# Low weight parts of a trunk block in one tile per 512 columns, each copied and loaded when the unit two places up has used it; the last norm's sum folded and moved up one unit

## The chip, the cores and the metric

The kernel runs on one core of one Trainium2 chip. The metric is device time in microseconds of one execution, from its first to its last instruction and what lies around them. Engines are called by the names of the profile: PE (TensorE, matmuls), PEld (its weight loads), DVE (VectorE), ACT (ScalarE), POOL (GpSimd), SP (SyncE, which issues most loads).

## The reference

One layer of a hybrid decoder on 528 tokens (16 learned ones and 512 of the input), width 1024:

```
h  = concat(meta, x)
p  = rmsnorm(h, norm1_g) @ w_in              # q k v glr r u ga gb
o  = rmsnorm(gla_chunked(q, k, v, log_a), gla_norm_g)
y_a = (o * silu(r)) @ w_a
y_b = (group_matmul(multiscale_pool(u)) * pool_scale) @ w_b
h  = h + (sigmoid(ga + b) * y_a + sigmoid(gb + b) * y_b) @ w_o
a, bv = split(causal_dwconv(rmsnorm(h, norm2_g) @ w_up))
h  = h + (silu(a) * bv) @ w_down             # D_FF = 2816
out = rmsnorm(h, final_norm_g)[16:]
```

All is float32. What matters here: the many weight matrices, and the norm at the very end, which needs the sum of squares over all 1024 channels of a token before anything can be stored.

## The kernel before

**Three products for one.** Each float32 operand of a matmul is split into a high part, rounded to the `F32R` type, and a low part, the rest; a product is high x high, high x low and low x high, three matmuls. Activations are stored with channels on the 128 partitions and tokens along the row. Weights come as units: a unit is 128 partitions x 4 blocks x 512 columns (a block holds four 128x128 weights).

**Order of units.** A list `seq` holds the units of the second phase (from about 187 us): u, a, ga, gb, grp, b, o, up and down, in an order written by hand. The first phase (q, k, v, r and the attention) has its own weights and is not touched. There are three kinds of units:

- *plain* (`plain`, `plain_half`): all three products of 256 output channels, in two halves `c` of 48 matmuls. Half 0 uses blocks 1 and 2 of the direct weights, half 1 block 0 and the weights of block 3 (`x`).
- *fast* (`fast`, `seven`): the same output by seven block products for eight (a Strassen-like scheme), each product twelve matmuls. Three use blocks 2, 0 and 1 of the direct weights (in this order: first, third, fifth product), four use sums of blocks (`sa`, `sb`, made by `make_sums`). The evictions to `z` stand on ACT and DVE between them.
- *down* (`down`): six or four weights for each of two output tiles.

**How a unit's weights are made.** SP loads the raw unit (`fetch`, three buffers, 1 MB). For unit n+1, during unit n, ACT makes the high part of three blocks (`make_high`, L631) and the sums are formed on DVE and split (`make_sums`, L650, L284, L285). The low part is made in one of two ways. For down, grp, b and o (`split_here`) DVE subtracts the high part from the raw one (L285, L633). For all others (`make_low`) ACT copies the negative of the *raw* three blocks, rounded, into the low tile (L621, one instruction of 128x1536), and then POOL issues three DMAs that add the exact weights to it from HBM, one per block (L623, `accum_op=ALU.add`). Low and high tiles have two buffers each, so the low tile of unit n+2 takes the place of unit n's; the copy must wait until PE has read that one. `make_low(n + 2)` is called from `prepare(n)` at the end of unit n, in fast units behind the eviction `turned` (L758) on ACT's queue.

Within an engine the instructions run in the order that the tile framework's scheduler gives them, which follows the order of the program and its own estimate of when each could start; `tc.issue_after` puts an instruction behind a given one on its engine.

**The end.** The last four down units (part 3 of D_FF) are computed for two halves of the tokens, `CUTS` of 256 columns, one after the other: for each `i` of four, two accumulations (`pe` L992), the addition to `h` (L1056, DVE), the square (L1057, ACT), the sum of squares `tot` (L1061, DVE) and the scaling with the norm's weights (L1066). `finish` of a half then sums over partitions with four matmuls against a float32 matrix of ones (`n3s`, L1029; two for `tot`, which holds two channel tiles side by side, two for the last square), makes the reciprocal root (L267, L269 on ACT, L271 to L273 on DVE), scales four pairs of tiles (L1036, DVE) and stores them. The first half's `finish` is called in the second half's loop at `i == 1`, the second's at the end.

Of the kernel before, what the change touches and what calls it, by code (L numbers as in the profile page):

```python
# [78 lines left out]
def hybrid_block(ctx: ExitStack, tc: tile.TileContext, xt, g1d, wts, wsq, wdown, wglr, wgk, vecs, out):  # L79
# [515 lines left out]
    def direct_tiles(n):  # L595
        if n not in own:
            fetch(n)
            job = seq[n]
            if n >= len(seq) - 2:
                hl = two(f"{n}")  # L600
                own[n] = hl, [t.rearrange("p a k n -> p (a k n)") for t in hl], 1024
                return own[n]
            hl = [gp.tile([P, 3, 512], F32R, tag=f"g{c}", name=f"g{c}{n}") for c in "hl"]
            if job[0] == "down":
                k = 2 * PARTS[job[1]][1] * P
                hl = [t.rearrange("p a b -> p (a b)")[:, 0:k] for t in hl]
                own[n] = [t.rearrange("p (c k n) -> p c k n", c=2, n=P) for t in hl], hl, k
            else:
                own[n] = [blocks(t) for t in hl], hl, None
# [5 lines left out]
    def make_low(n):  # L615
        if n >= len(seq) or split_here(n) or n in low_made:
            return
        low_made.add(n)
        _, (hi, lo), _ = direct_tiles(n)
        kind, name, i = seq[n]  # L620
        act.activation(lo, loaded[n][:, 0:3], AF.Copy, scale=-1.0)  # L621
        for b in (2, 0, 1) if kind == "fast" else (0, 1, 2) if name == "grp" else (1, 2, 0):
            pool.dma_start(lo[:, b], wsq[UNIT[name] + i, :, b], accum_op=ALU.add)  # L623

    def make_high(n):
# [3 lines left out]
        _, (hi, lo), k = direct_tiles(n)  # L629
        if k is None:  # L630
            act.activation(hi, loaded[n][:, 0:3], AF.Copy)  # L631
            if split_here(n):
                dve.tensor_tensor(lo, loaded[n][:, 0:3], f32(hi), ALU.subtract)  # L633
        else:
            split(hi, lo, loaded[n].rearrange("p a b -> p (a b)")[:, 0:k])
# [25 lines left out]
    def behind(ins, made, n):  # L661
        if ins is None:
            return made(n)
        with tc.issue_after(ins.ins):
            made(n)
# [12 lines left out]
    def plain_half(n, i, c, xh, xl, cols, w):  # L678
        g, x = w
        accs = [bank(f"pp{n}_{c}{h}") for h in range(2)]  # L680
        for k in range(KT):
            w = [
                (x[e][:, 0, k // 2] if k % 2 else g[e][:, 0, k // 2]) if c
                else g[e][:, 2 if k % 2 else 1, k // 2]
# [10 lines left out]
    def plain(n, i, xh, xl, cols, evict, cross=None):  # L695
# [3 lines left out]
        for c in range(2):  # L699
# [3 lines left out]
            elif cross is None or cross[0] is CROSS_X:  # L703
                spare(2)
        prepare(n)
# [14 lines left out]
    def seven(acc, w, block, x, at, n, first=True):  # L720
        for k in range(4):
            for e, (a, b) in enumerate(((0, 0), (0, 1), (1, 0))):
                pe.matmul(  # L723
                    acc[:, 0:n], w[a][:, block, k], x[k][b][:, at],
# [10 lines left out]
    def fast(n, z, sides, cols):  # L735
        direct, crossed = sides
        g, sa, sb = weights(n)
# [412 lines left out]
```

## Time and profile before

| | us |
|---|---|
| median of 3 runs (lowest, highest) | 831.64 (830.6, 833.38) |
| profiled execution | 833.59 |
| its span, first to last instruction | 831.8 |
| PE busy | 816.0 |
| DVE busy | 595.6 |
| ACT busy | 479.1 |
| POOL busy, 114 of its 149 instructions the DMA issues of L623 | 122.5 |

Busy time is the time in which an engine had an instruction running; the matmuls of PE overlap and their ends are modelled. The list of waits names for each idle stretch of an engine the instruction that waited, the one that released it, the total, the count and the longest. A timeline row has the start, the duration, the engine, the line and the operands, and in brackets how long the engine sat idle before. "To landing" is the time from a DMA's issue to its data having arrived.

### The profile page before, as it was taken

The numbers are of one execution on the slowest core, as the hardware profiler recorded it, in microseconds if no ns is written. First come the engines' busy times: TensorE is split into PE (matmuls) and PEld (weight loads), VectorE is DVE, ScalarE is ACT, GpSimd is POOL, SyncE is SP. The second block draws the span as 40 slices with busy tenths as digits, with TensorE's granted clock in tenths as the row PEclk, the third lists the DMA queues.
The fourth block names the chain that finished last, engine by engine and source line by source line (L and its number), as shares of the span: only waits on it lengthen the run. The fifth ranks groups of instructions, "written<-read, shape, count | busy, mean of one in ns | idle before, by whom it ended". The sixth has DMA issues, their size and how long they took to land.

```text
span 831.8 us, 15134 instructions
## 1 busy us (share of the span) xinstructions
PE 816.0 (98%) x6311; PEld 789.9 (95%) x6311; DVE 595.6 (72%) x891; ACT 479.1 (58%) x686; POOL 122.5 (15%) x149
## 2 busy tenths in 40 slices
PE   9999999999999999999999999999999999999995
PEld 7999999999999999999999999999989988999894
DVE  7677346679756797755564598998759965899845
ACT  7297244586655676644234457774557734786643
POOL 5000000021222122110003322220122110320000
PEclk9999999999999999999999999999999999999998
DMA  6423220248667777734342756875557644775102
GB/s 224 152 77 100 78 76 27 112 106 239 168 133 167 173 178 177 197 84 152 109 153 99 173 117 157 180 153 156 146 140 164 160 111 155 159 171 140 51 26 102
DMA packets 35861, 113.17 MB, mean 136 GB/s; under 512 B 3952, under 2 KB 7024, under 8 KB 29776
## 3 DMA queue, kind: packets, MB, share of 16 engines
q1 hardware_dynamic: 18688, 81.79, 29.9%
q0 software_dynamic: 16416, 29.89, 21.9%
q8 instruction: 49, 0.80, 0.4%
q10 hardware_dynamic: 688, 0.53, 0.2%
q14 instruction: 20, 0.16, 0.1%
HBM read 110.10 MB, written 2.10 MB: 135 GB/s over the span
## 4 chain that ended last, share of the span: by engine, by line
PE 84%; DMA 5%; DVE 5%; ACT 2%; issue 1%; POOL 1%; SPq 1%; DVEq 0%; ACTq 0%
PE pp L689 18%; PE x L723 14%; PE pd L992 12%; PE q L723 9%; PE pv L173 6%; PE y L723 5%; PE v L723 5%; PE pr L173 4%; DMA gl<-in_wsq_dram 4%; PE pq L173 3%; PE pe L992 2%; PE pgrp L851 1%; PE po L485 1%; PE po L484 1%; ACT gl L621 1%
## 5 line engine op out<-in xcount | busy, mean ns | idle before, releaser
L623 POOL DMA_DIRECT2D gl<-in_wsq_dram x114 | 102.0, 1212 | 500.0 <-ACT gl L621 430.2
L631 ACT ACTIVATE gh<-raw 128x1536 fp32r<-128x1536 f32 x47 | 69.8, 1486 | 61.4 <-PE pp L689 26.6
L650 DVE TENSOR_TENSOR raw<-raw 128x512 f32<-128x512 f32 x116 | 79.9, 689 | 26.8 <-ACT gh L631 14.5
L992 PE MATMUL pd<-g,gh 128*128 128x512 f32 x288 | 89.8, 393 | 0.0
L992 PEld LDWEIGHTS pd<-g,gh 128*128 128x128 f32 x288 | 53.8, 188 | 12.2
L621 ACT ACTIVATE gl<-raw 128x1536 fp32r<-128x1536 f32 x38 | 56.2, 1479 | 9.0 <-issue 4.5
L992 PE MATMUL pd<-g,gl 128*128 128x512 f32 x144 | 56.7, 394 | 0.0
L156 ACT ACTIVATE whi<-wraw 128x1024 fp32r<-128x1024 f32 (+2 forms) x28 | 26.1, 934 | 50.9 <-PE pv L173 25.8
L157 DVE TENSOR_TENSOR wlo<-wraw,whi 128x1024 fp32r<-128x1024 f32 (+2 forms) x28 | 32.0, 1145 | 5.7 <-ACT whi L156 4.5
L977 ACT ACTIVATE cv<-z,vec 128x512 f32<-128x512 f32 x44 | 33.9, 812 | 0.0
L992 PEld LDWEIGHTS pd<-g,gl 128*128 128x128 f32 x144 | 27.0, 188 | 6.1
L978 DVE SCALAR_TENSOR_TENSOR cv<-z,vec,cv 128x512 f32<-128x512 f32 x44 | 32.2, 746 | 0.0
L979 DVE SCALAR_TENSOR_TENSOR cv<-z,vec,cv 128x512 f32<-128x512 f32 x44 | 32.2, 746 | 0.0
L1017 DVE TENSOR_TENSOR h<-pd,h 128x512 f32<-128x512 f32 x24 | 16.5, 689 | 20.2 <-PE pd L992 20.0
L285 DVE TENSOR_TENSOR gl<-raw,gh 128x1536 fp32r<-128x1536 f32 (+1 forms) x14 | 23.5, 1679 | 6.1 <-ACT gh L284 6.1
L173 PE MATMUL pv<-xh,whi 128*128 128x264 f32 x128 | 26.3, 287 | 0.0
L173 PE MATMUL pr<-xh,whi 128*128 128x258 f32 (+1 forms) x128 | 25.9, 284 | 0.0
L173 PE MATMUL pv<-xl,whi 128*128 128x264 f32 x128 | 25.9, 283 | 0.0
L173 PE MATMUL pv<-xh,wlo 128*128 128x264 f32 x128 | 25.9, 283 | 0.0
L173 PE MATMUL pr<-xh,wlo 128*128 128x258 f32 (+1 forms) x128 | 25.8, 283 | 0.0
L173 PE MATMUL pr<-xl,whi 128*128 128x258 f32 (+1 forms) x128 | 25.6, 281 | 0.0
L284 ACT ACTIVATE gh<-raw 128x1536 fp32r<-128x1536 f32 (+1 forms) x14 | 19.9, 1422 | 5.1 <-PE pd L992 3.2
(1279 smaller groups left out, 2980.7 us busy)
## 6 DMA issues: line engine op xcount, KB each, us to landing
raw<-in_wsq_dram SPq DMA_DIRECT2D x47, 1024.0 KB, 5.7
gl<-in_wsq_dram POOLq DMA_DIRECT2D x114, 256.0 KB, 7.3
wraw<-in_wts_dram SPq DMA_DIRECT2D x22, 512.0 KB, 3.7
raw<-in_wdown_dram SPq DMA_DIRECT2D x12, 768.0 KB, 4.3
xb<-in_xt_dram SPq DMA_DIRECT2D x4, 528.0 KB, 5.1
h<-in_xt_dram SPq DMA_DIRECT2D x4, 514.0 KB, 5.1
raw<-in_wdown_dram SPq DMA_DIRECT2D x4, 512.0 KB, 3.5
x<-in_xt_dram SPq DMA_DIRECT2D x7, 264.0 KB, 5.6
```

The lines of the kernel that those rows point to most:

```text
L157: dve.tensor_tensor(lo[:, a:b], t[:, a:b], f32(hi[:, a:b]), ALU.subtract)
L173: pe.matmul(acc[:, s, : b - a], w, x[:, a:b], start=(i == 0 and w is wh and x is xh), stop=(i == n - 1 and last),)
L621: act.activation(lo, loaded[n][:, 0:3], AF.Copy, scale=-1.0)
L623: pool.dma_start(lo[:, b], wsq[UNIT[name] + i, :, b], accum_op=ALU.add)
L631: act.activation(hi, loaded[n][:, 0:3], AF.Copy)
L650: dve.tensor_tensor(raw[:, dst], raw[:, dst], raw[:, x], ALU.add)
L689: pe.matmul(acc[:, 0 : b - a], w[p], q[k][:, a:b], start=k == 0 and e == 0, stop=k == KT - 1 and e == 2,)
L723: pe.matmul(acc[:, 0:n], w[a][:, block, k], x[k][b][:, at], start=first and k == 0 and e == 0, stop=k == 3 and e == 2, skip_group_check=no ...
L977: act.activation(cv, z[:, c, META:], AF.Identity, scale=v1("cw2", m), bias=v1("cb", m))
L978: dve.scalar_tensor_tensor(cv, z[:, c, META - 1 : L - 1], v1("cw1", m), cv, ALU.mult, ALU.add)
L979: dve.scalar_tensor_tensor(cv, z[:, c, META - 2 : L - 2], v1("cw0", m), cv, ALU.mult, ALU.add)
L992: pe.matmul(acc, w[p][:, c, k], gated[k0 + k][q][:, a:b], start=k == 0 and e == 0, stop=k == nk - 1 and e == 2,)
```

## The change

Four edits, the first three for the low parts.

1. The low tile becomes three tiles of one block each (`gl0`, `gl1`, `gl2`, two buffers each, the same bytes in all); the weights are handed on as a function `piece(e, b, k)` in place of an array. Where DVE makes the low part, it does so in one subtraction per block (three instructions of 512 columns, two in the last part), and a down unit's two tiles are cut out of the blocks.
2. `make_low` takes the blocks to be made as an argument. Each block gets its own copy on ACT (128x512) and its own DMA right behind it, where before one copy of 128x1536 stood ahead of three DMAs.
3. In a fast unit n, block 2 of unit n+2 is made behind the eviction of `q` (L748), block 0 behind that of the second `x` (L751), and the rest in `prepare` as before; in a plain unit blocks 2 and 1 after half 0, block 0 in `prepare`.
4. At the end the sums of squares are folded into one tile: three further additions of 256 columns on DVE for the first half, two for the second. `finish` then has one matmul with the ones for the first half and two for the second, where both had four. The first half's `finish` is called at `i == 0`.

```diff
-            hl = [gp.tile([P, 3, 512], F32R, tag=f"g{c}", name=f"g{c}{n}") for c in "hl"]
...
+            hi = gp.tile([P, 3, 512], F32R, tag="gh", name=f"gh{n}")
+            lo = [gp.tile([P, 512], F32R, tag=f"gl{b}", name=f"gl{b}_{n}") for b in range(3)]
+            nk = PARTS[job[1]][1] if job[0] == "down" else 4
+
+            def piece(e, b, k):
+                b, k = divmod(b * nk + k, 4)
+                t = lo[b] if e else hi[:, b]
+                return t[:, k * P : (k + 1) * P]
...
-    def make_low(n):
-        if n >= len(seq) or split_here(n) or n in low_made:
+    def make_low(n, order=(2, 1, 0)):
+        if n >= len(seq) or split_here(n):
             return
-        low_made.add(n)
-        _, (hi, lo), _ = direct_tiles(n)
-        kind, name, i = seq[n]
-        act.activation(lo, loaded[n][:, 0:3], AF.Copy, scale=-1.0)
-        for b in (2, 0, 1) if kind == "fast" else (0, 1, 2) if name == "grp" else (1, 2, 0):
-            pool.dma_start(lo[:, b], wsq[UNIT[name] + i, :, b], accum_op=ALU.add)
+        lo = direct_tiles(n)[2]
+        for b in order:
+            if (n, b) not in low_made:
+                low_made.add((n, b))
+                act.activation(lo[b], loaded[n][:, b], AF.Copy, scale=-1.0)
+                pool.dma_start(lo[b], wsq[UNIT[seq[n][1]] + seq[n][2], :, b], accum_op=ALU.add)

     def make_high(n):
...
+        nb = -(-2 * PARTS[seq[n][1]][1] // 4) if seq[n][0] == "down" else 3
+        act.activation(hi[:, 0:nb], loaded[n][:, 0:nb], AF.Copy)
+        if split_here(n):
+            for b in range(nb):
+                dve.tensor_tensor(lo[b], loaded[n][:, b], f32(hi[:, b]), ALU.subtract)
...
@@ def plain
+            if c == 0:
+                make_low(n + 2, (2, 1))
         prepare(n)
...
@@ def fast
-        act.activation(z22, q[:, n_], AF.Copy)
+        behind(act.activation(z22, q[:, n_], AF.Copy), make_low, n + 2, (2,))
         seven(v_, g, 0, crossed, 3, w)
         seven(x, sa, 1, crossed, 2, w, False)
-        act.activation(z12, x[:, n_], AF.Copy)
+        behind(act.activation(z12, x[:, n_], AF.Copy), make_low, n + 2, (0,))
...
-    def finish(part, a, b, tot, last):
+    def finish(part, a, b, parts):
...
-        for e, x in enumerate((tot[:, 0], tot[:, 1], last[:, 0], last[:, 1])):
-            pe.matmul(s3[:, 0:w], ones32, x, start=e == 0, stop=e == 3)
+        for e, x in enumerate(parts):
+            pe.matmul(s3[:, 0:w], ones32, x, start=e == 0, stop=e == len(parts) - 1)
...
-            if i == 1 and late:
+            if i == 0 and late:
                 finish(*late)
...
+            if i == 2:
+                dve.tensor_tensor(tot[:, 0], tot[:, 0], tot[:, 1], ALU.add)
+            if i == 3:
+                dve.tensor_tensor(tot[:, 0], tot[:, 0], sq[:, 0], ALU.add)
...
-        late = part, a, b, tot, sq
+        if part < len(CUTS) - 1:
+            dve.tensor_tensor(tot[:, 0], tot[:, 0], sq[:, 1], ALU.add)
+            late = part, a, b, (tot[:, 0],)
+        else:
+            late = part, a, b, (tot[:, 0], sq[:, 1])
```

More of the change, by code (lines that the diff above doesn't have):

```diff
@@ L599, in direct_tiles @@
             if n >= len(seq) - 2:
-                hl = two(f"{n}")
-                own[n] = hl, [t.rearrange("p a k n -> p (a k n)") for t in hl], 1024
+                hi, lo = two(f"{n}")
+                own[n] = lambda e, c, k: (hi, lo)[e][:, c, k], hi, lo
                 return own[n]
-            hl = [gp.tile([P, 3, 512], F32R, tag=f"g{c}", name=f"g{c}{n}") for c in "hl"]
[L604 to L609, printed above, removed]
+            hi = gp.tile([P, 3, 512], F32R, tag="gh", name=f"gh{n}")
[5 more added lines that the diff above has]
+                return t[:, k * P : (k + 1) * P]
+            own[n] = piece, hi, lo
         return own[n]
@@ L628, in make_high @@
         high_made.add(n)
[L629 to L635, printed above, removed]
+        _, hi, lo = direct_tiles(n)
+        if n >= len(seq) - 2:
+            return split(hi, lo, blocks(loaded[n][:, 0:2]))
+        nb = -(-2 * PARTS[seq[n][1]][1] // 4) if seq[n][0] == "down" else 3
[3 more added lines that the diff above has]
+                dve.tensor_tensor(lo[b], loaded[n][:, b], f32(hi[:, b]), ALU.subtract)
     def two(name):
@@ L737, in fast @@
         g, sa, sb = weights(n)
+        sa, sb = (lambda e, b, k, t=t: t[e][:, b, k] for t in (sa, sb))
         z11, z12 = (z[:, 0, a:b] for a, b in cols)
```

16 lines of the change are left out of this document (8 added, 8 removed).

## The prediction

> **What bounds the kernel now.** I read the page first, for the busy engines, the clock and the chain that ended last; then the waits of TensorE (PE) and of its weight loads (PEld); then the timelines of the places that these waits name.
>
> ```profile
> span 831.8 us, 15134 instructions
> PE 816.0 (98%) x6311; PEld 789.9 (95%) x6311; DVE 595.6 (72%) x891; ACT 479.1 (58%) x686; POOL 122.5 (15%) x149
> PEclk9999999999999999999999999999999999999998
> PE 84%; DMA 5%; DVE 5%; ACT 2%; issue 1%; POOL 1%; SPq 1%; DVEq 0%; ACTq 0%
> ```
>
> PE is busy 98% of the span at the full granted clock and holds 84% of the chain. The change takes only a handful of matmuls away, so all it can win are PE's idle stretches and the tail behind the last matmul. The waits list the first:
>
> ```profile
> PE x L723 <- DMA gl<-in_wsq_dram: 1.5, 3, 1.1
> PE pp L689 <- DMA gl<-in_wsq_dram: 0.8, 1, 0.8
> PE q L723 <- ACT sh_10a L284: 0.8, 1, 0.8
> PE n2s L944 <- ACT n2hl L284: 0.4, 1, 0.4
> PE n2s L944 <- DVE n2hl L285: 0.2, 1, 0.2
> ...
> PEld x L723 <- DMA gl<-in_wsq_dram: 2.1, 3, 1.3
> PEld pp L689 <- DMA gl<-in_wsq_dram: 1.5, 3, 1.1
> PEld q L723 <- ACT sh_10a L284: 1.1, 1, 1.1
> PEld n2s L944 <- ACT n2hl L284: 0.6, 1, 0.6
> PEld n2s L944 <- DVE n2hl L285: 0.4, 1, 0.4
> ```
>
> Ends of matmuls are modelled, so the PE rows are the low side of a wait and the PEld rows (the weight that sits waiting) the high side. Waits for the low parts `gl` are 1.5 + 0.8 = 2.3 us by PE, 2.1 + 1.5 = 3.6 by PEld, six places in all; I take the middle, 2.9. `sh_10a` is 0.8 to 1.1, `n2s` 0.6 to 1.0. The rest of the span's middle has nothing that this change touches.
>
> **The change part by part.**
>
> *Copies and DMAs of the low parts.* A fast unit is seven groups of twelve matmuls. One whole unit, 543.43 to 553.53:
>
> ```profile
> 543.43:553.53 10.10, 10.10 (x86) 10.10 (x86) 9.79 (x16) 8.41 (x13) 2.65 (x3) 1.00 0.68 139
> ...
> 544.63 1.48 ACT L621 ACTIVATE gl<-raw 128x1536 fp32r<-128x1536 f32 x1
> ...
> 546.79 1.49 ACT L631 ACTIVATE gh<-raw 128x1536 fp32r<-128x1536 f32 x1
> 548.17 0.38 ACT L748 ACTIVATE z<-q 128x258 f32<-128x258 f32 x1
> 548.43 0.64 ACT L284 ACTIVATE g<-cv 128x512 fp32r<-128x512 f32 x1
> ...
> 549.66 0.39 ACT L751 ACTIVATE z<-x 128x258 f32<-128x258 f32 x1
> ...
> DMA to landing us min/median/max: 4.1/7.3/11.4
> ```
>
> The first row gives PE, PEld, DVE, ACT and POOL busy in that order. The copy at 544.63 serves the unit two places after the one that ended at 543.43; that unit starts at 553.53. The copy starts 1.2 us after its unit's end and takes 1.48, so the first accumulating DMA goes out some 7 us before its block is wanted. Landing takes 4.1 to 11.4: that spread on either side of 7 is the cause of the waits.
>
> For the unit n shown, the old copy comes behind its end at 553.53. After the change block 2 is copied behind L748 (548.17 + 0.38), inside it. With a copy of 128x512 at 0.64 (the row at 548.43) its DMA goes out near 549.2, and unit n+2 begins at 553.53 + 10.10 = 563.6: 14 us, against 11.4 for the slowest landing. Block 0 goes behind L751 (550.0 + 0.64), wanted in the third group, 16 us later; block 1 goes at the end, where the old copy stood, wanted in the fifth group of unit n+2. In a plain unit blocks 2 and 1 go after the first half, which gives about the same 15 us. Where the unit n+2 is plain and n is fast, block 1 is wanted at once and is still made at the end, but 1.48 - 0.64 = 0.84 earlier. So five of the six waits should vanish whole, and the sixth shrink by 0.84, more than it lasts. **Minus 2.9** (2.3 to 3.6).
>
> Cost on ACT: 3 x 0.64 - 1.48 = 0.44 per unit, at 38 units 17 us of work, at 8.41 of 10.10 us in the densest unit; the cover is ACT's idle time, and PE pays only where ACT feeds DVE too late (a rival below). What waits: the copy waits for the unit's own matmuls on that block, which have ended by then (it stands behind the eviction of a later group), and for its raw tile:
>
> ```profile
> raw<-in_wsq_dram SPq DMA_DIRECT2D x47, 1024.0 KB, 5.7
> ...
> 546.12 10.05 SPq L587 DMA_DIRECT2D raw<-in_wdown_dram  x2
> ...
> L285 DVE TENSOR_TENSOR gl<-raw,gh 128x1536 fp32r<-128x1536 f32 x12 | 21.1, 1755 | 5.7 <-ACT gh L284 5.7
> ...
> L650 DVE TENSOR_TENSOR raw<-raw 128x512 f32<-128x512 f32 x116 | 79.9, 689 | 26.8 <-ACT gh L631 14.5 <-ACT gl L621 10.5
> ...
> 385.00:465.00 80.00, 80.00 (x671) 79.79 (x670) 39.72 (x55) 29.00 (x35) 10.94 (x13) 1.00 0.41 126
> ```
>
> SP issues the raw tile of unit n+3 when the sums of unit n are done, early in unit n (546.12 in the unit shown); 5.7 us later, near 551.8, it is there, and the moved copy reads it in the next unit, at 548.55 + 10.10 = 558.7, 7 us on. Were it late, the evictions L751 and L758 would queue behind the copy on ACT. POOL sees the same three issues, spread out; the same 256 KB each. I put this at nothing: a landing may grow or shrink by some microseconds without PE seeing it while these margins last.
>
> *Low parts made on DVE* (down, grp, b, o): three subtractions of 512 for one of 1536, 3 x 0.689 - 1.755 = +0.31, 21 times. In b and o (385 to 465, the last row) DVE is busy 39.72 of 80. The first down of a pair is split inside a fast unit, where DVE has just 10.10 - 9.79 = 0.31 left; its matmuls come only after the rest of that unit. Nothing, at worst 5 x 0.31 = 1.5.
>
> *The sum of unit 10*, `sh_10a`:
>
> ```profile
> 298.15 1.48 ACT L621 ACTIVATE gl<-raw 128x1536 fp32r<-128x1536 f32 x1
> 299.52 1.05 ACT L284 ACTIVATE sh_10a<-raw 128x1024 fp32r<-128x1024 f32 x1
> ```
>
> It stands right behind the old copy on ACT. With one block left there it starts 0.84 earlier. **Minus 0.85** (0 to 1.1).
>
> *The second norm's sum*, `n2s`:
>
> ```profile
> 464.87 1.47 ACT L621 ACTIVATE gl<-raw 128x1536 fp32r<-128x1536 f32 x1
> ...
> 467.79 1.95 POOL L883 TENSOR_TENSOR n_sq<-n_sq,n_sq 128x514 f32<-128x514 f32 x1
> ...
> 466.99 0.75 DVE L879 SCALAR_TENSOR_TENSOR h2l<-h,vec,h2h 128x514 fp32r<-128x514 f32 x1 [1.92 <-ACT h2h L878]
> 468.04 2.27 DVE L285 TENSOR_TENSOR sl_26x<-raw,sh_26x 128x512 fp32r<-128x512 f32 x1 [0.29 <-ACT sh_26x L284]
> ```
>
> The old copy at 464.87 holds ACT before h2h and the square, which feed POOL's last sum and then `n2hl`. One block instead of three brings that chain 0.84 forward; a remainder of 0.1 is left for the second pair. **Minus 0.7** (0 to 1.0). The lower end is this: beside POOL's sum a DVE subtraction of 512 took 2.27 against 0.69 alone, so the two engines hold each other up, and POOL's sum, now earlier, could lose L879's 0.75. The Trainium skill, SBUF — State Buffer, section "SBUF: two separate sides", calls the port pair of DVE and GpSimd an exclusive lock: a DVE instruction with two SBUF inputs and a GpSimd instruction that reads SBUF do not run together, and the later one blocks for the whole of the first. The 2.27 agrees with that. By the rule, should L879 start first, the sum below is 5.45 instead of 6.15.
>
> *The last norm.*
>
> ```profile
> 795.61 17.13 PE pe L992 x144
> 812.73 1.74 PE n3s L1029 x8
> ...
> 819.87 0.28 PE L992 MATMUL pe<-g,sl 128*128 128x256 f32 x1
> 821.23 1.97 PE L1029 MATMUL n3s<-n_sq,ones 128*128 128x256 f32 x8 [1.08 <-DVE n_sq L1061]
> ...
> 817.99 2.49 DVE L1036 TENSOR_TENSOR h<-h,r 128x512 f32<-128x512 f32 x4
> 821.00 0.75 DVE L1056 TENSOR_TENSOR h<-pe,h 128x256 f32<-128x256 f32 x2
> 821.45 0.75 ACT L1057 ACTIVATE n_sq<-h 128x256 f32<-128x256 f32 x2 [1.77 <-DVE h L1056]
> 823.23 0.47 ACT L267 ACTIVATE r<-n3s,eps_t 128x256 f32<-128x256 f32 x1 [0.64 <-PE n3s L1029]
> ```
>
> Each fp32 matmul with the ones is two rows, four of them 8 rows, 0.22 a row (1.74 / 8). Part 0 keeps two rows of eight: PE ends 6 x 0.22 = 1.3 earlier, its last matmul starting at 818.57 instead of 819.87. Today DVE is then still at the four L1036 of part 0 (817.99 to 820.48) and a sum of squares behind them, and takes up the last eviction only at 821.00. Moved up by one unit (24 matmuls, 17.13 / 6 = 2.86 us), these are through before 816.5, so the eviction follows the last matmul's start by its 0.28 and a few hundredths, at 818.90. Then eviction 0.45 (821.45 - 821.00), square 0.45, the new addition 0.47 (an estimate, half a 128x512 and its wait), and four rows of n3s for eight: 2.00 - 0.88 = 1.12 (2.00 is 823.23 - 821.23, 0.88 four rows). L267 starts at 818.90 + 0.45 + 0.45 + 0.47 + 1.12 = 821.4, against 823.23: 1.8. I take **minus 1.7**; if DVE is as busy as today at that point, 0.9. The other new additions, part 0's, lie beside matmuls. Behind L267 all stays.
>
> Sum: 2.9 + 0.85 + 0.7 + 1.7 = 6.15. The profiled execution took 833.59, 1.8 more than its span and 1.95 more than the median of 831.64; some of its DMA waits may be longer than the median's, one more reason for 2.9 and not 3.6. From the median: 831.64 - 6.15 = **825.5**.
>
> **Rivals.**
>
> *Only the loads and the tail.* ACT or the two engines' holding each other up keeps `sh_10a` and `n2s`, and 2.9 + 1.7 = 4.6 is won: 827.0. For it: both terms rest on one place each, and on the order that the scheduler draws for ACT and DVE. The same time, within 1 us, comes out if the copies end up where they were, for even then block 2 leaves 0.84 earlier and no wait but the longest outlasts that.
>
> *Only the tail.* The landings grow as they now fall in with the raw tiles' 1 MB, or small waits for sums take the place of those for `gl`: 831.64 - 1.7 = 829.9. Against it: the margin rises from 7 to 14 us, above the longest landing.
>
> *DVE overruns, slower.* In a fast up unit DVE has 9.79 of 10.10. Its sums for the next unit stand behind the conv's pieces, which wait for ACT (L284 at 548.43 and L977 after it). The two copies now in mid-unit, 2 x 0.64, get ahead of these. If DVE stands idle more than 0.31 for it, PE waits for `sl` in each of 18 fast up units: with both copies in the way (1.28 - 0.31) x 18 = 17.5, less 6.15, gives 843; the turn to slower comes at 0.31 + 6.15 / 18 = 0.65, one copy. Against it: the high copy L631, and the sums behind it, begin 0.84 earlier, as the old copy ahead of it shrinks; ACT is as far as today when it reaches 548.43.
>
> **How the numbers follow.** Forecast 0.55, loads and tail only 0.25 (both faster), tail only 0.13 (within 0.3%, which is about what a measurement of this kernel can tell from no change, 2.5 us), DVE overrun 0.07. Faster 0.80, same 0.13, slower 0.07. The best ends, 3.6 + 1.1 + 1.0 + 1.8 = 7.5, give 824.1; with the scatter of runs I set the low end at 823.5. The high end is 830.0, at the case of the tail only: left out are 0.07, half of that case and a little below, together some 0.17.
>
> **What would show it.** Right: no row "PE <- DMA gl" among the waits, or tenths; L623 spread over the unit; L267 of part 1 about 1.8 us after the last "pe" matmul's end plus the chain above, with no L1036 between; `n3s` twice less than half as long. Wrong: new PE rows for `sl` or `sh` of the sums, landings above 11.4, DVE full in the up units, ACT waiting for raw tiles.

## The result, and the profile after

| | before | changed |
|---|---|---|
| median, us | 831.18 | 825.73 |
| lowest and highest of 6 runs each | 830.6, 833.38 | 825.35, 826.93 |
| ratio of the two, 95% interval | | 0.9932, 0.992 to 0.9944 |
| profiled execution (its span) | 833.59 (831.8) | 826.93 (825.2) |

The change wins 5.45 us by the medians and 6.66 by the two profiled executions: the profile of before was taken of an execution 2.4 us above its median, that of the changed kernel of one 1.2 above. The page of the changed kernel:

```profile
PE 811.3 (98%) x6301; PEld 787.2 (95%) x6301; DVE 597.0 (72%) x940; ACT 488.8 (59%) x762; POOL 121.7 (15%) x149
PEclk9999999999999999999999999999999999999997
PE 94%; DVE 2%; DMA 1%; ACT 1%; SPq 1%; issue 0%; POOL 0%; DVEq 0%; ACTq 0%
...
L625 ACT ACTIVATE gl<-raw 128x512 fp32r<-128x512 f32 x114 | 70.9, 627 | 37.4 <-PE pd L999 23.0
```

PE now holds 94% of the chain that ended last, where it held 84%; the 5% of DMA and 5% of DVE have shrunk to 1% and 2%. ACT pays for it with 114 copies of 0.627 us (70.9 us in all), out of its idle time. One digit is new: the granted clock ends on 7, not 8. The waits of PE, the whole list:

```profile
PE n3s L1036 <- DVE n_sq L1072: 2.0, 1, 2.0
PE heat L204 <- POOL warm L201: 1.4, 1, 1.4
PE pk L173 <- ACT xh L246: 0.6, 1, 0.6
PE n1s L294 <- DVE sq L263: 0.4, 1, 0.4
PE pk L173 <- DVE xl L247: 0.3, 1, 0.3
PE pk L173 <- ACT whi L156: 0.3, 1, 0.3
```

Every row that the change aimed at is gone: no `gl`, no `sh_10a`, no `n2s`. What is left is the start (`heat`, `pk`, `n1s`) and one wait at the end, for the last norm's sum, that is longer than before. The landing of the 256 KB DMAs, least, median and most, of before had a median of 7.3 us; here:

```profile
DMA to landing us min/median/max: 3.9/5.4/10.8
```

**A fast up unit after the change**: first a stretch of one unit's length in the view of busy time (length, then PE, PEld, DVE, ACT and POOL, each with its count, then clock, DMA share and GB/s); then from the timeline the unit's first matmul on PE, ACT's high copy, its moved copies and the sum behind them. Below it, rows of the same unit in the kernel before:

```profile
539.40:549.50 10.10, 10.10 (x86) 10.10 (x86) 10.01 (x17) 8.59 (x15) 2.59 (x3) 1.00 0.75 159
...
537.76 0.28 PE L729 MATMUL x<-dh,gh 128*128 128x258 f32 x1
...
539.92 1.48 ACT L636 ACTIVATE gh<-raw 128x1536 fp32r<-128x1536 f32 x1
...
542.09 0.62 ACT L625 ACTIVATE gl<-raw 128x512 fp32r<-128x512 f32 x1
...
544.29 0.62 ACT L625 ACTIVATE gl<-raw 128x512 fp32r<-128x512 f32 x1
544.90 1.06 ACT L284 ACTIVATE sh_33a<-raw 128x1024 fp32r<-128x1024 f32 x1
545.87 0.62 ACT L988 ACTIVATE cv<-cv 128x512 f32<-128x512 f32 x1
```

```profile
543.27 0.28 PE L723 MATMUL x<-dh,gh 128*128 128x258 f32 x1
...
546.00 0.62 ACT L981 ACTIVATE cv<-cv 128x512 f32<-128x512 f32 x1
...
551.02 1.06 ACT L284 ACTIVATE sh_33a<-raw 128x1024 fp32r<-128x1024 f32 x1 [0.27 <-DVE raw L650]
```

`sh_33a` started 551.02 - 543.27 = 7.75 us into the unit and starts 544.90 - 537.76 = 7.14 into it now, 0.6 earlier, though two copies have been put ahead of it. Part of this is the order that the scheduler drew: before, ACT took a piece of the conv (L981, 0.62) ahead of the high copy, and now it takes that piece (L988) behind the sum.

**The second norm**, by the timeline of the changed kernel:

```profile
461.94 0.61 ACT L625 ACTIVATE gl<-raw 128x512 fp32r<-128x512 f32 x1
...
463.85 1.29 POOL L890 TENSOR_TENSOR n_sq<-n_sq,n_sq 128x514 f32<-128x514 f32 x1
...
464.25 1.44 DVE L285 TENSOR_TENSOR sl_26x<-raw,sh_26x 128x512 fp32r<-128x512 f32 x1 [0.29 <-ACT sh_26x L284]
465.84 0.70 DVE L285 TENSOR_TENSOR n2hl<-n_sq,n2hl 128x514 fp32r<-128x514 f32 x1
...
467.00 0.63 PE L951 MATMUL n2s<-n2hl,ones 128*128 128x258 f32 x4
```

From the copy's start to POOL's sum it is 463.85 - 461.94 = 1.9 us, against 467.79 - 464.87 = 2.9 before, and the sum's parts are ready at 466.54, 0.46 before PE takes them up.

**The end**, PE, DVE and ACT in the timeline:

```profile
812.33 0.28 PE L999 MATMUL pe<-g,sl 128*128 128x256 f32 x1
814.62 1.80 PE L1036 MATMUL n3s<-n_sq,ones 128*128 128x256 f32 x4 [2.02 <-DVE n_sq L1072]
...
806.82 2.50 DVE L1043 TENSOR_TENSOR h<-h,r 128x512 f32<-128x512 f32 x4
809.24 1.28 DVE L1063 TENSOR_TENSOR h<-pe,h 128x512 f32<-128x512 f32 x2
810.62 0.69 DVE L1068 TENSOR_TENSOR n_sq<-n_sq,n_sq 128x512 f32<-128x512 f32 x1
812.09 0.69 DVE L1068 TENSOR_TENSOR n_sq<-n_sq,n_sq 128x512 f32<-128x512 f32 x1 [0.77 <-ACT n_sq L1064]
812.81 0.42 DVE L1070 TENSOR_TENSOR n_sq<-n_sq 128x256 f32<-128x256 f32 x1
813.15 0.75 DVE L1063 TENSOR_TENSOR h<-pe,h 128x256 f32<-128x256 f32 x2
...
816.46 0.47 ACT L267 ACTIVATE r<-n3s,eps_t 128x256 f32<-128x256 f32 x1 [1.71 <-PE n3s L1036]
```

From the start of the last `pe` matmul to L267 it is now 816.46 - 812.33 = 4.13 us; before it was 823.23 - 819.87 = 3.36. PE has less to do there, and the chain behind it is longer. Two things stand out: the last evictions start 813.15 - 812.33 = 0.82 after the last matmul, and four rows of `n3s` take 1.80, where eight took 1.97.

**By stage.** The start times of matmuls in each trace split the span at two marks, the first `pp` matmul (unit u0) and the first `pe` matmul (the last four down units). The stretch between them (the middle) took 608.08 us before and 601.22 after; from the first `pe` to the end (the tail) it took 36.40 and 36.00. So 6.86 came from the middle and 0.40 from the tail; the start, which the change doesn't touch, was 0.6 longer in this execution. The same two stretches are given for each experiment below.

### The profile page after: what moved, and what is told of

The parts are those of the page before. It is cut to its first block, busy times and chain, and to the rows that moved or that the text cites. A ratio compares the mean times of both kernels' runs of the same rounds, so it can differ in the third digit from the quotient of the medians.

```text
span 825.2 us, 15267 instructions
## 1 busy us (share of the span) xinstructions
PE 811.3 (98%) x6301; PEld 787.2 (95%) x6301; DVE 597.0 (72%) x940; ACT 488.8 (59%) x762; POOL 121.7 (15%) x149
## 4 chain that ended last, share of the span: by engine, by line
PE 94%; DVE 2%; DMA 1%; ACT 1%; SPq 1%; issue 0%; POOL 0%; DVEq 0%; ACTq 0%
PE pp L693 24%; PE x L729 15%; PE pd L999 12%; PE q L729 10%; PE pv L173 6%; PE pr L173 6%; PE y L729 5%; PE v L729 5%; PE pq L173 3%; PE pe L999 2%; PE pgrp L858 1%; PE po L485 1%; PE po L484 1%; DMA x<-in_xt_dram 1%; PE pk L173 1%; DMA wraw<-in_wts_dram 1%
## 5 line engine op out<-in xcount | busy, mean ns | idle before, releaser
L626 POOL DMA_DIRECT2D gl<-in_wsq_dram x114 | 98.9, 897 | 499.6 <-ACT gl L625 249.7
L636 ACT ACTIVATE gh<-raw 128x1536 fp32r<-128x1536 f32 (+1 forms) x61 | 89.8, 1472 | 53.0 <-PE pp L693 30.1
L625 ACT ACTIVATE gl<-raw 128x512 fp32r<-128x512 f32 x114 | 70.9, 627 | 37.4 <-PE pd L999 23.0
L639 DVE TENSOR_TENSOR gl<-raw,gh 128x512 fp32r<-128x512 f32 x67 | 46.2, 720 | 8.1 <-ACT gh L636 7.8
L157 DVE TENSOR_TENSOR wlo<-wraw,whi 128x1024 fp32r<-128x1024 f32 (+2 forms) x28 | 30.0, 1075 | 6.3 <-ACT whi L156 5.1
L870 DVE TENSOR_TENSOR gb<-pp,gb 128x258 f32<-128x258 f32 (+1 forms) x16 | 6.1, 421 | 24.2 <-PE pp L693 24.2
```

The costliest lines, as they stand in the source:

```text
L625: act.activation(lo[b], loaded[n][:, b], AF.Copy, scale=-1.0)
L626: pool.dma_start(lo[b], wsq[UNIT[seq[n][1]] + seq[n][2], :, b], accum_op=ALU.add)
L636: act.activation(hi[:, 0:nb], loaded[n][:, 0:nb], AF.Copy)
L639: dve.tensor_tensor(lo[b], loaded[n][:, b], f32(hi[:, b]), ALU.subtract)
```

## The experiments

Theory: the middle is won by the earlier copies and DMAs, and it is won whole; the tail wins less than the matmuls it saves, since DVE is behind when the last matmul ends and the clock may fall while PE waits. Rivals: that the copies' length does it and not their place; that the copies get in DVE's way in the fast units; that what the tail lacks is DVE's backlog alone. The experiments were run in three groups, each with its own runs of the kernel before, whose medians were 832.03 (low_only, norm_only, split_in_place, pe_kept_busy), 831.66 (in_place_order, after_again, stores_spread, spread_busy) and 831.59 (the other four). With the 831.18 of the first comparison these differ by 0.85, so a difference of that size between two groups says nothing. The middle and the tail come from one profiled execution each.

| kernel | median | ratio to before, 95% | middle | tail |
|---|---|---|---|---|
| before | 831.18 | 1 | 608.08 | 36.40 |
| changed | 825.73 | 0.9932 (0.992 to 0.9944) | 601.22 | 36.00 |
| low_only | 826.58 | 0.9932 (0.9911 to 0.9953) | 601.17 | 36.55 |
| norm_only | 830.79 | 0.9979 (0.9962 to 0.9997) | 608.03 | 35.15 |
| split_in_place | 829.66 | 0.9971 (0.9958 to 0.9983) | 605.37 | 35.50 |
| in_place_order | 828.43 | 0.9963 (0.9949 to 0.9977) | 604.17 | 36.37 |
| fast_only | 825.60 | 0.9924 (0.9909 to 0.9939) | 601.18 | 36.21 |
| plain_only | 829.61 | 0.9986 (0.9966 to 1.0005) | 605.86 | 35.53 |
| copy_twice | 825.14 | 0.9917 (0.9899 to 0.9935) | 601.18 | 35.12 |
| copies_all_twice | 825.25 | 0.9922 (0.9907 to 0.9938) | 601.20 | 36.07 |
| after_again | 826.06 | 0.9935 (0.9923 to 0.9947) | 601.23 | 35.88 |
| pe_kept_busy | 825.47 | 0.9917 (0.9897 to 0.9938) | 601.23 | 35.31 |
| stores_spread | 825.15 | 0.9927 (0.9915 to 0.9939) | 602.36 | 34.81 |
| spread_busy | 825.03 | 0.9923 (0.991 to 0.9936) | 601.23 | 34.83 |

Every kernel that has the moved copies in the fast units took 601.2 in the middle, but for one wait in stores_spread (below). That is the floor of this order of matmuls; in the changed kernel no row of PE waits there. The ratio of plain_only is nearer to 1 than its median because two of its twelve executions took 835.65 and 836.02; the others took 828.95 to 830.42.

### The two halves of the change apart

low_only takes the changed kernel and undoes edit 4; norm_only puts edit 4 alone into the kernel before.

```diff
 # low_only, against the changed kernel
-        for e, x in enumerate(parts):
+        for e, x in enumerate((tot[:, 0], tot[:, 1], last[:, 0], last[:, 1])):
...
-            if i == 0 and late:
+            if i == 1 and late:
...
-            if i == 2:
-                dve.tensor_tensor(tot[:, 0], tot[:, 0], tot[:, 1], ALU.add)
...
-            late = part, a, b, (tot[:, 0], sq[:, 1])
+        late = part, a, b, tot, sq
```

> The low parts' edits alone, the last norm as before. My theory now, from the two traces: PE's idle places in the middle (waits for gl, sh_10a and n2s) are all gone, about 5.1 us of the 5.45, and the norm's edit gives only some 0.4 because its n3s rows run at half the granted clock. Then this kernel is 5.0 us faster than before, about 826.1, and its tail reads as before's: n3s twice in 1.7 to 2.0 us, L267 of the second half 3.4 us after the last pe matmul. Rival, the prediction as written: middle 4.45, tail 1.7; then this one is 826.7 to 827.5, and the rest of the 5.45 is the norm's.

> The last norm's edit alone, the low parts as before. My theory now: 1.3 us less of n3s on PE, 0.9 given back since PE stands idle for 2 us ahead of the second n3s and the granted clock falls to a half there: 0.3 to 0.6 us faster than before, about 830.7. The waits for gl, sh_10a and n2s stay as before. Rival, the prediction as written: 1.7 us faster, 829.5.

low_only is 5.45 under the runs of before beside it, with the middle at its floor and the tail as before. norm_only is 1.24 under them, and its interval reaches from 0.25 to 3.2 us; its middle is that of before to 0.05, its tail 1.25 shorter. So the low parts are worth about 5.5 of the medians, and the norm some 1.2 by this execution's tail. Its time came as its expectation had it (about 830.7), but not for the reason given there, a clock that falls to a half ahead of `n3s`: here the clock stayed and four rows of `n3s` took 1.10 (last section). In the changed kernel the norm seems to give less, 826.58 - 825.73 = 0.85, or 0.52 by after_again, but these compare different groups and are not settled.

### The copies split, but left in place

split_in_place keeps the tiles of one block and drops the three moved calls, so that blocks 2, 1 and 0 are all made at the unit's end. in_place_order does the same in the old order of blocks.

```diff
 # split_in_place, against the changed kernel
-            if c == 0:
-                make_low(n + 2, (2, 1))
...
-        behind(act.activation(z22, q[:, n_], AF.Copy), make_low, n + 2, (2,))
+        act.activation(z22, q[:, n_], AF.Copy)
...
-        behind(act.activation(z12, x[:, n_], AF.Copy), make_low, n + 2, (0,))
+        act.activation(z12, x[:, n_], AF.Copy)
 # in_place_order, besides
-    def make_low(n, order=(2, 1, 0)):
+    def make_low(n):
+        order = (2, 0, 1) if seq[n][0] == "fast" else (1, 2, 0)
```

> The changed kernel with the block copies and their DMAs left at the end of the unit: three tiles and three short copies, but no copy moved up. My theory: moving is what the gl waits needed (landing up to 11 us against some 7 us of room), splitting alone brings block 2 only 0.84 us forward; so the longest gl waits (1.3 and 1.1) keep 0.2 to 0.5 each, sh_10a and n2s stay gone or short, and the time is 0.5 to 1.0 above the changed kernel, 826.2 to 826.8. Rival: splitting alone does it, the landings being shorter once the three DMAs no longer go out together; then within 0.3 of the changed kernel, and no row of PE waiting for gl. Other rival: three copies in a row at the unit's end are longer than one (1.9 against 1.48), sh_10a and z11 are later: above 827.

> As split_in_place (three short copies and DMAs, all at the end of the unit), with the blocks in the old order (2, 0, 1 for fast units, 1, 2, 0 for plain ones). The run before had 2, 1, 0 and so new waits of the third product for block 0 (1.0 to 1.4 us by the list). Theory: these go, the first blocks still come late now and then; 828.0 to 828.8, some 1 to 1.5 us faster than split_in_place, 2.3 to 3 slower than the changed kernel. Rival 1, splitting alone is enough once the order is right: within 0.5 of the changed kernel. Rival 2, the order is no matter: 829.7.

The first of these expectations missed: splitting wins 2.7 of the 6.9 us of the middle, not nearly all. The second was met (828.43). The waits of split_in_place show a new place:

```profile
PE v L727 <- DMA gl<-in_wsq_dram: 1.0, 2, 0.7
PE pp L693 <- DMA gl<-in_wsq_dram: 0.8, 1, 0.8
```

`v` is the third product of a fast unit, on block 0, which in the order 2, 1, 0 is now the last to go out. With the old order the row of `v` is gone and the middle 1.2 shorter (604.17), but three waits for `x` are there, of 0.6 at most. So by these traces shorter copies alone are worth 608.08 - 604.17 = 3.9, the new order costs 1.2 of that where the copies stay in place, and the rest, 605.37 - 601.2 = 4.2, comes from the places. The 1.2 rests on one execution of each: the intervals of the two ratios overlap.

### Which of the moved calls

fast_only keeps the moved calls of the fast units, plain_only those of the plain ones.

```diff
 # fast_only, against the changed kernel
-            if c == 0:
-                make_low(n + 2, (2, 1))
 # plain_only, against the changed kernel
-        behind(act.activation(z22, q[:, n_], AF.Copy), make_low, n + 2, (2,))
+        act.activation(z22, q[:, n_], AF.Copy)
...
-        behind(act.activation(z12, x[:, n_], AF.Copy), make_low, n + 2, (0,))
+        act.activation(z12, x[:, n_], AF.Copy)
```

> The changed kernel with the moves in plain units undone: there blocks 2, 1 and 0 are all made at the end of the unit, one copy and one DMA after the other; the fast units keep both moved calls. Theory (each wait for a weight goes where its block is made earlier): the waits of the fast units and of sh_10a stay away, those that follow plain units (three of the six of before, and n2s, whose chain stood behind a copy of three blocks) may return in part, each under 0.8 us as the first block's copy is shorter: 0.5 to 2 us slower than the changed kernel, 826.0 to 828.0. Rival (the place does not matter, the scatter of landings does): as the changed kernel within 0.5 us, 825.3 to 826.3.

> The changed kernel with the two moved calls in fast units undone: there blocks 2, 1 and 0 are all made in prepare at the end of the unit; plain units keep their moved call. Theory: the waits that follow fast units return in part, with block 0 (wanted third) now last of three: PE waits of 0.5 to 2.5 us in all and a further slot of 0.11 at each, 827.0 to 829.0, and fast_only and plain_only together lose about what split_in_place lost (3.9 us against the changed kernel, by medians). Rival (the moves in fast units do nothing): 825.3 to 826.3.

What the places give, the moves in the fast units give alone. fast_only ran as the changed kernel did (825.60, the rival of its expectation) and plain_only as split_in_place (829.61 against 829.66; the expected 827 to 829 was too low). The three rows that plain_only shows for `gl`:

```profile
PE v L729 <- DMA gl<-in_wsq_dram: 1.1, 1, 1.1
PE pp L693 <- DMA gl<-in_wsq_dram: 0.8, 1, 0.8
PE x L729 <- DMA gl<-in_wsq_dram: 0.8, 2, 0.6
```

By their starts (255.1, 297.5, 300.9 and 750.0 us) they stand in units whose low parts were made during a fast unit; the one of `pp` is the plain unit a3, two places behind the fast u1. The waits that before had behind plain units (224.2 and 211.7, units a2 and a1) went with the shorter copies in all of these kernels. The median landing is 7.0 us in plain_only and 5.4 in fast_only: in this kernel the landing itself is shorter where the three DMAs don't leave together.

### Is ACT's idle time the cover?

copy_twice does block 2's copy in each fast unit twice; copies_all_twice does all three twice. The second copy writes what the first wrote.

```diff
 # copies_all_twice; in copy_twice the condition is: if order == (2,)
                 act.activation(lo[b], loaded[n][:, b], AF.Copy, scale=-1.0)
+                if seq[n - 2][0] == "fast":
+                    act.activation(lo[b], loaded[n][:, b], AF.Copy, scale=-1.0)
```

> The changed kernel with block 2's copy in each fast unit done twice, so ACT has one more instruction of 0.62 us there, ahead of what the conv and the sums need from it: ACT 8.59 to about 9.2 of the 10.10 us of a fast up unit. Theory (ACT's idle time covers it, the sums are formed 0.9 us earlier than before the change and have that to lose): within 0.5 us of the changed kernel, 825.2 to 826.5, DVE idle no longer than before. Rival (DVE overruns once copies stand ahead of the conv's evictions, turning at 0.65 us more of idle time in each unit): 0.3 to 0.6 us in each of 18 fast up units, 831 to 836.

> The changed kernel with all three copies done twice in fast units: ACT 8.59 + 3 x 0.62 = 10.45 us of work in a fast up unit of 10.10. Theory: the cover is gone here and ACT becomes the bound, 0.3 to 1 us for each of the 18 fast up units: 831 to 844, clock still near full, PE waits for sums (sa, sb) or their low parts. If the cover were something else than ACT's idle time (say, slack of the sums over a whole unit), it would stay under 829.

Neither cost anything (825.14 and 825.25, middle 601.18 and 601.20). For copy_twice that was the theory. For copies_all_twice it was not: 831 to 844 was expected. A unit's length of copies_all_twice, and two rows of ACT in it, a copy and what follows:

```profile
539.40:549.50 10.10, 10.10 (x87) 10.10 (x86) 10.04 (x17) 10.04 (x18) 2.59 (x3) 1.00 0.74 156
...
549.10 0.62 ACT L625 ACTIVATE gl<-raw 128x512 fp32r<-128x512 f32 x1
549.62 0.63 ACT L990 ACTIVATE cv<-cv 128x512 f32<-128x512 f32 x1
```

ACT is full here, 10.04 of 10.10, and just keeps up. The expectation added 3 x 0.62 to 8.59; but an ACT row starts 0.52 after the one before it (549.62 - 549.10), not 0.62, so three copies are 1.55 and the sum 10.14, which the row shows as all but the whole unit. It was also wrong in the number of units: only ten of the 18 fast up units make copies, as the unit two places behind the other eight is a down unit, and of the ten only four (units 31, 32, 42 and 52) are as full as this. The rival that DVE overruns once copies stand in its way is false at all sizes tried: up to six copies in a fast unit PE waits for no sum. But no run took ACT's room away altogether, so what happens beyond is not shown, and neither is whether ACT's idle time alone was the cover or the slack of the sums over a whole unit helps, which that expectation names as the reading of a time under 829.

### The tail

pe_kept_busy gives PE twelve matmuls on a spare bank between the last `pe` matmul and `n3s`, so that it is not idle for so long. stores_spread takes the four L1043 of part 0 out of `finish` and puts two each behind the evictions of `i` = 1 and 2. spread_busy does both.

```diff
 # pe_kept_busy
+            if part == len(CUTS) - 1 and i == 3:
+                idle = bank("idle")
+                for _ in range(12):
+                    pe.matmul(idle[:, 0:w], ones, gated[FF - 1][0][:, a:b], start=True, stop=True)
 # stores_spread (store(i) is the body of the loop of L1043 and its DMA)
-                finish(*late)
+                store = finish(*late)
...
-                dve.tensor_tensor(h[:, c], both[:, c], h[:, c], ALU.add)
+                held = dve.tensor_tensor(h[:, c], both[:, c], h[:, c], ALU.add)
+            if store and i in (1, 2):
+                with tc.issue_after(held.ins):
+                    for k in (2 * i - 2, 2 * i - 1):
+                        store(k)
```

> The changed kernel with twelve matmuls into an unused bank between the last pe matmul and the second n3s (1.4 us of PE in what were 2.0 idle). If the fall of the granted clock is what makes n3s slow (four rows in 1.81), it stays at 1.00 until n3s is through, the four rows take 0.9 and the kernel is 0.9 us faster than the changed one, about 824.8. Rival: n3s is slow for another reason, or the clock falls all the same: no change, 825.7.

> The changed kernel itself, run beside the next three so that they are compared on one chip. About 825.7. If its second n3s falls in a stretch at full granted clock this time (four rows in 1.1 instead of 1.8), the tail is 0.7 shorter than in its first profile: the theory is that the idle 2 us ahead of n3s let the clock fall in some executions and not in others. Rival: the clock falls in every execution of this kernel.

> The changed kernel with the first half's four scalings (L1043 on DVE) and their stores put two behind the eviction of i = 1 and two behind that of i = 2, instead of all four ahead of both. Theory: in the changed kernel these four (2.5 us in one block) keep DVE and then ACT half a microsecond behind PE, so that the last eviction starts 0.8 after the last matmul and not 0.33. Spread out, it starts at 0.35, and the kernel is 0.5 us faster than the changed one in the same call; PE's idle time ahead of the second n3s is 1.5 and not 2.0, which also makes a fall of the clock rarer (up to 0.7 more). Rival: the chain of additions behind the last eviction sets the end whatever DVE did before: no change.

> Both the spread scalings and the twelve matmuls into an unused bank ahead of the second n3s. If the two causes (DVE behind by 0.5, clock falling by chance, 0.7 when it does) are separate, 0.5 to 1.2 us faster than the changed kernel, the fastest of all here: 824.6 to 825.2. Rival: the extra matmuls are in n3s's way once PE's idle time is only 1.5: then no faster than the spread alone.

With PE kept busy, the clock stays and four rows of `n3s` take 1.10 (0.9 was expected); here in pe_kept_busy:

```profile
811.38 1.60 PE L1061 MATMUL idle<-g,ones 128*128 128x256 f32 x12
813.55 1.10 PE L1036 MATMUL n3s<-n_sq,ones 128*128 128x256 f32 x4 [0.58 <-DVE n_sq L1076]
```

The tail goes from 36.00 to 35.31. The expected 824.8 was not reached: the median, 825.47, is 0.26 under the changed kernel's, in another group, which settles nothing. In after_again, the changed kernel once more, the clock fell again and the four rows took 1.71.

In stores_spread, DVE, PE and ACT at the end:

```profile
813.35 0.75 DVE L1065 TENSOR_TENSOR h<-pe,h 128x256 f32<-128x256 f32 x2
...
813.00 0.28 PE L999 MATMUL pe<-g,sl 128*128 128x256 f32 x1
814.82 1.10 PE L1036 MATMUL n3s<-n_sq,ones 128*128 128x256 f32 x4 [1.54 <-DVE n_sq L1078]
...
815.96 0.47 ACT L267 ACTIVATE r<-n3s,eps_t 128x256 f32<-128x256 f32 x1 [1.02 <-PE n3s L1036]
```

The eviction now follows the last matmul by 813.35 - 813.00 = 0.35, as the prediction had it (0.33), and `n3s` starts 1.82 behind that matmul, where it was 2.29. The tail is 34.81, 1.59 shorter than before and 1.19 shorter than in the changed kernel. Not all of the 1.19 is the scalings': the clock stayed in this execution. From the last `pe` matmul to L267 it is 815.96 - 813.00 = 2.96, and 821.87 - 818.44 = 3.43 in norm_only, which has the changed tail and in whose execution the clock stayed too. So the spread scalings give 0.47, and the rest is the clock. By the medians stores_spread is 0.91 under after_again in its group, with five executions each whose ranges overlap (824.93 to 826.42 and 825.70 to 826.57).

The middle of stores_spread has one wait for `gl`, of 0.9 us at 255.50. It is at the plain unit a3, two places behind the fast u1: its block 1 is still made at the end of u1 and wanted at once. The DMA went out at 245.96 and landed 9.5 us later; in the other kernels with the moved copies this landing took 6.3 to 7.5, in the changed one 7.2 from 246.43, wanted at 254.88. The room at this place is 254.88 - 246.43 = 8.45 us, so a landing as slow as that one would make the changed kernel wait there too. No execution on record of it shows that.

spread_busy was the fastest of the study: 825.03, four runs from 824.73 to 825.44, all below the five of after_again in its group (825.70 to 826.57). Beyond that pair it is not settled: the intervals against before overlap, and copy_twice and copies_all_twice, which have the changed kernel's own tail, had 825.14 and 825.25 in another group.

## Why the prediction was right

**The time and its cause.** 825.5 was forecast, 825.73 came, and the mechanism is the one named: the blocks leave earlier, the margin against the landing grows, PE stops waiting. Its share by place is another than the prediction gave: the moves in the fast units do what it said, in the plain units the shorter copies were enough. Two terms of the sum were off, in opposite directions: the middle gave about 1 us more (5.5 by the medians for 4.45), and the tail less than the 1.7 taken in every execution profiled. The gain was 5.45 where the sum had 6.15, and it was taken from 831.18 where the sum started at 831.64. That the total came within 0.25 is in part luck.

**The middle was sized too small**: 2.9 + 0.85 + 0.7 = 4.45, where the same profiled execution gave 6.86 and the medians about 5.5. The step that failed is reading the cost of a wait off the list of waits. Two waits of the kernel before, with the matmuls around them:

```profile
297.78 0.28 PE L723 MATMUL x<-dlx,gh 128*128 128x264 f32 x1
298.29 0.39 PE L723 MATMUL x<-dhx,gl 128*128 128x264 f32 x1 [0.23 <-DMA gl<-in_wsq_dram]
298.52 0.29 PE L723 MATMUL x<-dhx,gh 128*128 128x264 f32 x1
298.64 0.28 PE L723 MATMUL x<-dlx,gh 128*128 128x264 f32 x1
...
299.49 0.28 PE L723 MATMUL x<-dhx,gl 128*128 128x264 f32 x1
300.62 0.39 PE L723 MATMUL q<-xxh,sh_10a 128*128 128x264 f32 x1 [0.85 <-ACT sh_10a L284]
300.85 0.29 PE L723 MATMUL q<-xxl,sh_10a 128*128 128x264 f32 x1
```

Matmuls start 0.12 apart (298.52 to 298.64) but their rows are 0.28 long, since they overlap. The list counts idle time from the modelled end of the row before, so it leaves out 0.28 - 0.12 = 0.16; and the matmul after the one that waited starts 0.23 on, not 0.12, another 0.11. The first wait cost 298.29 - 297.78 - 0.12 + 0.11 = 0.50 and is listed with 0.23; the second 300.62 - 299.49 - 0.12 + 0.11 = 1.12 and is listed with 0.85. **A wait costs its PE row and 0.27.** Each of the seven waits that the list has in the middle of before cost 0.26 to 0.28 more than its row: 3.80 us by the rows, 5.66 by the starts of matmuls, each step against the median of the same step over all kernels of the table. The remaining 1.2 of the 6.86 stands in no row of the list: it is made of steps that are long by one slot of about 0.11 or a little more, 0.23 at most. The changed kernel has none of either kind. The PEld rows, taken as the high side, count about 0.2 of the 0.27.

The remark that this execution's waits may be longer than the median's fits: it ran 2.4 above the later medians of before, and by the medians the term is about 5.5. The places of the waits for `gl` are a draw as well. norm_only, whose low parts are those of before, waited at 213.15, 257.16, 299.07 and 502.69, before at 224.20, 298.29, 533.30 and 637.84; `sh_10a` and `n2s` waited in both. So "five of the six waits should vanish whole, and the sixth shrink by 0.84, more than it lasts" goes by the places and sizes of one execution: the sixth, at a3, was long by 0.23 in before and waited 0.9 in stores_spread. The remark under the first rival, that copies left in place give 827.0 within 1 us, missed: in_place_order took 828.43 and split_in_place 829.66.

**`sh_10a` and `n2s`** went whole, as forecast. The fear for `n2s`, that POOL's sum would lose 0.75 to L879 (now L886), did not come true: POOL's sum starts at 463.85, 1.9 behind the copy, and takes 1.29, less than the 1.95 of before. L886 ran from 463.21 to 463.96 and was all but through by then, so this run does not show what it would have cost in the middle of POOL's sum. That the two engines hold each other up still shows in `sl_26x`, 1.44 us beside POOL's sum against 0.69 alone; it ends at 465.69, 0.55 behind POOL's sum, as before (470.31 and 469.74, 0.57). So the sum of 6.15 was the one to use and not 5.45.

**The tail was sized too large**: 1.7 was taken, 0.40 came in the profile of the changed kernel. Against the 36.40 of before the changed tail won 0.87 to 1.28 in the four profiled executions in which the clock stayed, and 0.03 to 0.52 in the five in which it fell. That PE ends 1.3 earlier was right: from the first `pe` to the last it was 24.42 and is 23.11. The step that failed is "these are through before 816.5, so the eviction follows the last matmul's start by its 0.28 and a few hundredths". The four L1043 are through, 3.0 before the last matmul starts (806.82 + 2.50 against 812.33); but they held up two evictions, these two sums of squares, the second of which waits for ACT, and these the fold L1070, and the queue is still being worked off when the last matmul ends. The eviction comes 0.82 behind the last matmul's start, 0.49 late. A further 0.10 is in the steps from there to `n3s` (814.62 - 813.15 = 1.47 for 1.37), and 0.72 in `n3s` to L267 (816.46 - 814.62 = 1.84 for 1.12), because the clock fell. stores_spread takes the first away (0.47 by its rows) and pe_kept_busy the last (36.00 to 35.31, 0.69).

**The costs put at nothing** were nothing. ACT has 8.59 of 10.10 in the fast unit for 8.41, DVE 10.01 for 9.79; copies_all_twice shows how much more was free on ACT. The argument against the slower rival, that the high copy and the sums begin earlier, holds: the high copy begins 539.92 - 537.76 = 2.16 into its unit for 546.79 - 543.27 = 3.52, which is the 0.84 of the shorter copy and about 0.5 by the conv's piece L988 that no longer stands ahead of it, and `sh_33a` begins 0.6 earlier (the expectation of copy_twice has 0.9). The second part is the scheduler's order, which the prediction did not name. That rival also counted 18 fast up units, of which only ten make copies.

## What to carry to other kernels

When a wait for a load is to go, give the load a place by the unit's own clock and try each place alone: here the two calls in fast units did all that the places gave, and splitting the copy without moving it gave 2.7 to 3.9 of 6.9 us, by the order of the blocks. Price a stall of PE by the start times on both sides of it, not by the list of waits, which left out 0.27 us of each. And before an addition or a sum is counted as hidden, follow the whole queue that a moved block holds up, not the block itself; a tail of four scalings was through in time, and five instructions behind it were not.

## What the runs showed of the hardware

**The clock falls on a grid.** In the trace's record of the granted clock it is full for 808.96 us in the changed kernel, from 5.92 to 814.88; in norm_only for 819.20 us, from 4.35 to 823.55; in the kernel before for 819.20, in others for 812.37 or 815.78. These times differ by 3.41 us or a multiple of it, and are 237, 240, 238 and 239 times 3.4133 us. Two ends of the grid, in the view by stretch, first of the changed kernel and then of norm_only:

```profile
811.47:814.88 3.41, 1.39 (x11) 1.21 (x10) 2.47 (x6) 2.64 (x7) 0.00 (x0) 1.00 0.08 26
814.88:816.42 1.54, 1.54 (x4) 0.68 (x3) 0.00 (x0) 0.00 (x0) 0.00 (x0) 0.50 0.00 0
```

```profile
816.72:820.13 3.41, 2.00 (x17) 1.79 (x16) 2.48 (x5) 2.75 (x7) 0.00 (x0) 1.00 0.32 114
820.13:823.55 3.42, 1.10 (x4) 0.68 (x4) 1.38 (x4) 1.62 (x4) 0.00 (x0) 1.00 0.00 0
```

Both kernels have the same idle stretch of 2.0 us ahead of the last `n3s`. In the first the stretch falls so that PE is busy 1.39 of 3.41 us by the rows; the clock is 0.50 in the next stretch, and `n3s` takes 1.80. In the second PE is busy 2.00 of 3.41, the clock stays, and `n3s` takes 1.10; it falls at the end of the next stretch, with 1.10 of 3.42 busy. So between 1.39 and 2.00 us busy of 3.41 lies what decides in these traces. Of the nine profiled executions with this idle stretch the clock fell ahead of or in `n3s` in five (tails 35.88 to 36.37) and not in four (35.12 to 35.53): some 0.8 us on the average, by the chance of where the grid lies. The Trainium skill, TensorE: Matmul & The Clock Gate, section "Part 1: The HAM clock gate (the "warmup" mystery)", gives a free-running window of 3413 ns, and the multiples agree. It puts the slow state after at least one idle window; here 2.0 us of idle time in a window were enough, and the measurement decides.

**ACT's rows overlap.** Two instructions of 0.62 start 0.52 apart, so the cost of one more is 0.10 less than its row. The Trainium skill, ScalarE: Activation LUTs, section "What ACT_TABLE_LOAD costs", has activations back to back overlap by about 93 ns, which agrees; had the sum for copies_all_twice been made so, ACT would have come out at about the unit's length, and not 0.35 over it.
